# Gate LoRA and twelve head sums as fp32r products of parts, in a hybrid GDN and RWKV-7 decoder block

## The chip, the cores and the metric

The kernel runs on one core of one Trainium2 chip. The core has five engines with an instruction stream each: TensorE (PE in the profile; PEld is its weight load), VectorE (DVE), ScalarE (ACT), GpSimd (POOL) and SyncE (SP, which issues most of the DMAs). The metric is the device time of one execution in microseconds, as the median over several runs. Before the change it is 935.27 us (three runs, 934.57 to 936.5).

## The reference

The program computes one decoder block on 512 tokens of width 1024, all in float32. Two token mixers run in parallel on the same normed input (a gated DeltaNet, "GDN", and an RWKV-7 time mix, eight heads of 64 each), are merged by sigmoid gates, and a ConvGLU channel mixer follows. These are the parts that the change touches:

```python
# RWKV-7 time mix
g = jax.nn.sigmoid(g_lo) @ f32(g2)                     # gate LoRA: 160 -> 512
kk = l2_normalize(heads(k * f32(k_k)))                 # a sum of squares over each head
...
mean = jnp.mean(y, axis=-1, keepdims=True)
var = jnp.mean(jnp.square(y - mean), axis=-1, keepdims=True)
y = ((y - mean) * lax.rsqrt(var + LNX_EPS)).reshape(B, T, RWKV_WIDTH) * f32(lnx_w) + f32(lnx_b)
bonus = jnp.sum(r * k * f32(r_k), axis=-1, keepdims=True) * v   # a sum over each head
return (y + bonus.reshape(B, T, RWKV_WIDTH)) * g
# gated DeltaNet, its end
o = rms_norm(o, onorm_w) * jax.nn.silu(heads(z).astype(jnp.float32))   # a mean of squares over each head
```

## The kernel before, in words

**Layout.** Activations lie transposed: a tile has 128 feature rows and T = 512 tokens as columns. A width of 512 (eight heads of 64) is four such column tiles, counted by `ct`; one tile holds two heads. A sum over a head is therefore a matmul with a 128x128 matrix `ones_bd` that has ones in its two diagonal blocks of 64: every row of the result holds its head's sum.

**Precision.** TensorE multiplies fp32 operands as they are, or "fp32r" operands, which are rounded. Where fp32r is used, an operand is split into parts: `split(hi, lo, src, eng)` lets ScalarE cast `src` to `hi` (L145) and another engine subtract, `lo = src - hi` (L148). A projection's product is then three fp32r matmuls, hi·hi, hi·lo and lo·hi (L186, L189, L190). A head sum has exact ones, so `block_sum` (L168 to L175) needs two, with `hi` (L174) and with `lo` (L175). Before the change `block_sum` is used for the eight sums of the layer norm at the end of the RWKV mixer only, with GpSimd for the subtraction. All other head sums, and the gate LoRA, are fp32 matmuls, each of which shows as two rows of PE in the trace.

**Fills.** The large projections stand in a queue. `fill(n)` puts the next n k-tiles of that queue (three matmuls each, L186 to L190) between the steps of a chain, so that TensorE has work while another engine is at the chain. Weights come by DMA from SyncE into `raw` (two buffers), are cast by ScalarE into `whi` (L145) and subtracted by VectorE into `wlo` (L148), two buffers of each. The adaLN vectors are VectorE reductions over a streamed weight (`wada`, L209), spread over the same time.

**What sets the order.** Every engine runs its own stream in order. The framework lays the program's calls into these streams by its own estimate of when operands are ready, so that an added instruction can move others on its engine and elsewhere. Temporaries come from rings: `tmp(tag)` and `tmp_r(tag)` with the same tag share two buffers ("sq", "sp", "acc", "sg", "rs"), and a third request waits until the first one's readers are done.

**The stages around the change.** (1) Until about 212 us the first projections, the GDN's chunk matrices and a triangular solve (`solve`, L594 and L604 on TensorE, L571 and L573 on VectorE). Just before its last steps the gate's hidden values are passed through a sigmoid, in `sg2` (128 rows) and `sg3` (32 rows; L707 and L708). (2) The GDN recurrence over eight chunks (L774 to L817, about 226 to 300 us): per chunk small products (L181), with VectorE's `cz` (L785), `ck` (L793) and `cs` (L807) and ScalarE's `cv` between them. Between its steps, `more(n)` runs a piece of `prepare()` (L718 to L762), which readies the RWKV operands tile by tile: square of k (L732), head sum (L742), reciprocal root on ScalarE, then products on VectorE and GpSimd (L745 to L758), and the bonus' head sum (L760). (3) Chunk products of RWKV (L843, to 311 us), then the four head sums over the GDN output `go` (L857 to L864), the SiLU of z, the product with it, and the `bg` projection that needs it. (4) The RWKV solve and scan (to 457 us), with fills between. (5) The layer norm loop (L947 to L967, about 458 to 486 us): per tile a sum, a square, a second sum, the scale, and the gate product of two fp32 matmuls: 128 rows of g2 with `sg2` (L963) and 32 rows with `sg3` (L964). (6) Projections to the end.

Of the kernel before, what the change touches and what calls it, by code (L numbers as in the profile page):

```python
# [23 lines left out]
T = 512  # L24
# [31 lines left out]
def body(ctx, tc, io, out, tap=lambda name, ap: None):  # L56
# [298 lines left out]
    p = pa()  # L355
# [59 lines left out]
    lora = ct4(slot(11))  # L415
    lo1, w2, a2, wt = lora[:, 0], lora[0:65, 1], lora[:, 2], lora[0:65, 3]
    sg2 = const.tile([128, T], F32, name="sg2")
    sg3 = const.tile([32, T], F32, name="sg3")
    sp.dma_start(w2, io["w2"])
    sp.dma_start(a2[64:128], io["a2"])  # L420
    pool.memset(wt[64:65], 1.0)
# [22 lines left out]
    p = first_ps[0]  # L444
    ba = tmp("rs")
    act.copy(ba[32:64], p[32:64])
    token_shift(sg3, p, col("mu_lo", 2), omu[:, 14:15], 32)
    for j in range(4):
        gkq(0, j)(first_ps[1 + j])
        if j < 2:  # L450
# [254 lines left out]
    fill(2)  # L705
    table(SIG)
    fn(sg2, sg2, AF.Sigmoid)  # L707
    fn(sg3, sg3, AF.Sigmoid)  # L708
    for b in range(4):
        p = pa()  # L710
        pe.matmul(p, wt[:, 128 * b:128 * b + 128], w2, start=True, stop=True)
# [11 lines left out]
    def prepare():  # L723
        for ct in range(4):
            p = pa()
            pe.matmul(p, a2[64:128, 128 * ct:128 * ct + 128], lo1[64:128], start=True, stop=True)
            fn(aa[:, ct], p, AF.Sigmoid, bias=col("a0", ct))
            yield
        table(EXP)
        for ct in range(4):  # L730
            sq = tmp("sq")
            act.activation(sq, rk_[:, ct], AF.Square, scale=col("k_k", ct))  # L732
            p = pa()
            for b in range(4):
                pe.matmul(p[:, 128 * b:128 * b + 128], lw[:, b, 128 * ct:128 * ct + 128], cumtri,
                          start=True, stop=True)
            pinc, pi = tmp("acc"), tmp("sg")
            fn(pinc, p, AF.Exp)
            fn(pi, p, AF.Exp, scale=-1.0)
            yield  # L740
            p = pa()
            pe.matmul(p, ones_bd, sq, start=True, stop=True)  # L742
            kk = tmp("rs")
            rstd_of(p, 1.0, kk)
            dve.scalar_tensor_tensor(kk, rk_[:, ct], col("k_k", ct), kk, op0=ALU.mult, op1=ALU.mult)  # L745
            pool.tensor_copy(ch(ar[:, 0, ct])[:, :, 0:1], ch(kk)[:, :, 0:1])
            pool.tensor_copy(pend[:, ct], ch(pinc)[:, :, C - 1])
            dve.tensor_tensor(ch(ar[:, 0, ct])[:, :, 1:], ch(kk)[:, :, 1:], ch(pinc)[:, :, 0:C - 1], op=ALU.mult)
            pool.tensor_tensor(kk, aa[:, ct], kk, op=ALU.mult)
            yield  # L750
            t = tmp("sq")
            dve.tensor_scalar(t, aa[:, ct], col("k_a", ct), oka[:, ct:ct + 1], op0=ALU.mult, op1=ALU.add)
            dve.tensor_tensor(rk_[:, ct], rk_[:, ct], t, op=ALU.mult)
            dve.tensor_tensor(aa[:, ct], kk, pi, op=ALU.mult)

            dve.scalar_tensor_tensor(t, rk_[:, ct], col("r_k", ct), rr_[:, ct], op0=ALU.mult, op1=ALU.mult)
            pool.tensor_tensor(rk_[:, ct], pi, rk_[:, ct], op=ALU.mult)
            dve.tensor_tensor(rr_[:, ct], rr_[:, ct], pinc, op=ALU.mult)  # L758
            p = pa()
            pe.matmul(p, ones_bd, t, start=True, stop=True)  # L760
            act.copy(bonus[:, ct], p)
            yield  # L762

# [93 lines left out]
    for ct in range(4):  # L857
        sq = tmp("sq")
        act.activation(sq, go[:, ct], AF.Square)
        p = pa()  # L860
        pe.matmul(p, ones_bd, sq, start=True, stop=True)
        rs = tmp("rs")
        rstd_of(p, 1.0 / C, rs)
        dve.scalar_tensor_tensor(go[:, ct], go[:, ct], col("onorm"), rs, op0=ALU.mult, op1=ALU.mult)  # L864
# [71 lines left out]
    tap("ry", ry)  # L936


    g2s = slot2(2)
    g2a, g2b = g2s[:, 0:T], g2s[0:32, T:2 * T]  # L940
    sp.dma_start(g2a, io["g2"][0:128])
    sp.dma_start(g2b, io["g2"][128:160])
    table(EXP)
    sig_in[0] = False
    rb_h, rb_l = quarter(slot(2, F32R)), quarter(slot(12, F32R))
    for ct in range(4):
# [13 lines left out]
        dve.scalar_tensor_tensor(t, t, col("lnx_w", ct), rs, op0=ALU.mult, op1=ALU.mult)  # L960
        dve.scalar_tensor_tensor(t, t, col("lnx_b", ct), bonus[:, ct], op0=ALU.add, op1=ALU.add)
        p = pa()
        pe.matmul(p, g2a[:, 128 * ct:128 * ct + 128], sg2, start=True, stop=False)  # L963
        pe.matmul(p, g2b[:, 128 * ct:128 * ct + 128], sg3, start=False, stop=True)  # L964
        dve.tensor_tensor(t, t, p, op=ALU.mult)
        split(rb_h[ct], rb_l[ct], t)
        fill(2)  # L967
# [256 lines left out]
```

## Time and profile before

The profiled execution took 937.31 us; its span, from the first to the last instruction, is 935.6 us, at a mean granted clock of 0.983.

| what | before |
|---|---|
| median of the runs | 935.27 us |
| profiled execution, its span | 937.31 us, 935.6 us |
| TensorE busy | 876.3 us (94%), 5459 matmul rows |
| VectorE, ScalarE, GpSimd busy | 533.3, 419.2, 95.2 us |
| fp32 head sums in `prepare()` (L742, L760) | 8, in 232 to 300 us |
| fp32 head sums over `go` (L861) | 4, in 311 to 325 us |
| fp32 gate matmuls (L963, L964) | 8, in 458 to 486 us |

A row of the page's groups or of a view by line has: line, engine, operation, output<-inputs, shape, count | busy us, mean ns of one | idle time of the engine just before, and what ended it. A row of the waits has: engine, what it was about to do <- the engine and instruction that it waited for: us in total, times, longest. A row of the chain or the timeline begins with its start and its length in us. Matmul rows overlap, since TensorE is pipelined; the distance from one start to the next tells what a matmul costs, not its length.

### The profile page before, as it was taken

The page shows a single profiled execution, that of the slowest core. Times are in us where ns is not written, and L with a number is a line of the kernel's source. Part 1 is how long each engine was busy: PE and PEld are TensorE (multiplying, and loading weights), DVE is VectorE, ACT ScalarE, POOL GpSimd, SP SyncE. Part 2 cuts the span into 40 slices and gives each one's busy share as a digit, 9 for nine tenths or more (in the row PEclk, how much of TensorE's full clock was granted, in tenths as well). Part 3 has the DMA queues.
Part 4 walks back from the last instruction along what each step waited for, and adds up shares of the span by engine and source line. Part 5 has one row for each costly group of instructions (what it writes and reads, how often), then busy time and mean ns, then how long its engine had stood idle before and what let it go on. Part 6 is the DMA issues. An engine that isn't in the chain of part 4 may idle for free.

```text
span 935.6 us, 13853 instructions
## 1 busy us (share of the span) xinstructions
PE 876.3 (94%) x5459; PEld 687.7 (74%) x5459; DVE 533.3 (57%) x858; ACT 419.2 (45%) x680; POOL 95.2 (10%) x91
## 2 busy tenths in 40 slices
PE   2999999999989978899999999999999999999996
PEld 1886577677656666677668888888888888888885
DVE  5987859824696786255476537564445445332233
ACT  5367543734554747632465335343333333333231
POOL 1000300000352300001230120000000000010112
PEclk9999999997999989899999999999999999999998
DMA  9841245363323367644546542322322322533322
GB/s 332 283 149 67 91 105 185 109 166 112 103 82 113 69 213 267 162 147 148 183 158 202 171 141 84 111 91 92 109 92 90 105 99 90 179 98 100 107 80 91
DMA packets 81119, 125.72 MB, mean 134 GB/s; under 512 B 26045, under 2 KB 42813, under 8 KB 80990
## 3 DMA queue, kind: packets, MB, share of 16 engines
q1 hardware_dynamic: 81054, 124.83, 42.2%
q8 instruction: 43, 0.70, 0.3%
q14 instruction: 22, 0.18, 0.1%
HBM read 110.13 MB, written 14.16 MB: 133 GB/s over the span
## 4 chain that ended last, share of the span: by engine, by line
PE 69%; DVE 10%; DMA 6%; ACT 6%; issue 6%; POOL 2%; SPq 0%; DVEq 0%; POOLq 0%; ACTq 0%
PE ps_mm L186 19%; PE ps_mm L189 18%; PE ps_mm L190 18%; DMA wada<-in_w_ada 4%; DVE wlo L148 2%; PE ps_pc L181 2%; DVE wada L209 1%; ACT tmp_rs L94 1%; PE ps_pc L186 1%; PE ps_pc L189 1%; PE ps_pc L190 1%; ACT slot L619 1%; PE ps_pa L186 1%; PE ps_pa L189 1%; PE ps_pa L190 1%
## 5 line engine op out<-in xcount | busy, mean ns | idle before, releaser
L186 PE MATMUL ps_mm<-hh,whi 128*128 128x512 f32 (+1 forms) x642 | 264.2, 412 | 9.8 <-ACT hh L308 3.4
L148 DVE TENSOR_TENSOR wlo<-raw,whi 128x1024 fp32r<-128x1024 f32 (+2 forms) x140 | 161.2, 1152 | 176.2 <-ACT whi L145 170.6
L190 PE MATMUL ps_mm<-hh,wlo 128*128 128x512 f32 (+1 forms) x642 | 255.0, 399 | 1.3 <-DVE wlo L148 1.3
L189 PE MATMUL ps_mm<-hl,whi 128*128 128x512 f32 (+1 forms) x642 | 253.8, 396 | 0.0
L145 ACT CAST whi<-raw 128x1024 fp32r<-128x1024 f32 (+2 forms) x140 | 137.1, 979 | 259.7 <-PE ps_mm L189 198.4
L186 PEld LDWEIGHTS ps_mm<-hh,whi 128*128 128x128 f32 x642 | 121.5, 190 | 46.8 <-issue 8.5
L190 PEld LDWEIGHTS ps_mm<-hh,wlo 128*128 128x128 f32 x642 | 121.6, 189 | 31.6 <-issue 3.4
L189 PEld LDWEIGHTS ps_mm<-hl,whi 128*128 128x128 f32 x642 | 122.1, 190 | 26.7 <-issue 4.0
L186 PE MATMUL ps_mm<-slot,whi 128*128 128x512 f32 (+1 forms) x226 | 85.7, 379 | 4.7 <-ACT tmp_sp L94 4.7
L190 PE MATMUL ps_mm<-slot,wlo 128*128 128x512 f32 (+1 forms) x226 | 85.1, 376 | 0.0
L189 PE MATMUL ps_mm<-slotd,whi 128*128 128x512 f32 (+1 forms) x168 | 62.4, 371 | 0.0
L186 PEld LDWEIGHTS ps_mm<-slot,whi 128*128 128x128 f32 x226 | 43.2, 191 | 12.6 <-ACT tmp_sp L94 4.9
L190 PEld LDWEIGHTS ps_mm<-slot,wlo 128*128 128x128 f32 x226 | 43.1, 191 | 7.7
L189 PE MATMUL ps_mm<-slot,whi 128*128 128x512 f32 (+1 forms) x122 | 45.3, 372 | 0.0
L186 PE MATMUL ps_mm<-slotd,whi 128*128 128x512 f32 (+1 forms) x96 | 36.4, 379 | 0.0
L190 PE MATMUL ps_mm<-slotd,wlo 128*128 128x512 f32 (+1 forms) x96 | 36.1, 376 | 0.0
L209 DVE CUSTOM_DVE_ANT_0 wada<-wada,cond,cols 128x512 f32<-128x512 f32 x32 | 25.6, 800 | 18.3 <-DMA wada<-in_w_ada 18.2
L189 PEld LDWEIGHTS ps_mm<-slotd,whi 128*128 128x128 f32 x168 | 31.6, 188 | 5.7
L1099 DVE TENSOR_TENSOR tmp_sg<-tmp_acc,ps_mm 128x512 f32<-128x512 f32 x20 | 13.8, 688 | 36.0 <-PE ps_mm L190 35.8
L209 DVE CUSTOM_DVE_ANT_0 wada<-wada,cond,half 128x512 f32<-128x512 f32 x32 | 24.9, 779 | 14.6 <-DMA wada<-in_w_ada 14.4
L398 DVE SCALAR_TENSOR_TENSOR tmp_acc<-ps_mm,cols,tmp_acc 128x511 f32<-128x511 f32 (+2 forms) x44 | 32.8, 746 | 0.7
L1032 POOL COPY tmp_rs<-tmp_sq 128x512 f32<-128x512 f32 x2 | 2.1, 1064 | 304.0 <-ACT tmp_sq L1029 304.0
(270 smaller groups left out, 1262.5 us busy)
## 6 DMA issues: line engine op xcount, KB each, us to landing
raw<-in_w_in SPq DMA_DIRECT2D x40, 512.0 KB, 4.1
raw<-in_w_fi SPq DMA_DIRECT2D x37, 512.0 KB, 3.5
wada<-in_w_ada SPq DMA_DIRECT2D x64, 256.0 KB, 2.7
raw<-in_w_fo SPq DMA_DIRECT2D x16, 512.0 KB, 3.6
slot<-in_w_ada SPq DMA_DIRECT2D x10, 512.0 KB, 8.5
slot<-in_xT SPq DMA_DIRECT2D x16, 256.0 KB, 4.6
raw<-in_w_out SPq DMA_DIRECT2D x8, 512.0 KB, 3.4
raw<-in_w_in SPq DMA_DIRECT2D x8, 448.0 KB, 4.5
```

The costliest lines, as they stand in the source:

```text
L94: i = act.activation(*a, **k)
L145: i = act.copy(hi, src)
L148: j = eng.tensor_tensor(lo, src, hi.bitcast(F32), op=ALU.subtract)
L181: last["step"] = pe.matmul(*a, **k)
L186: i = pe.matmul(p, hi, xh, start=start, stop=False)
L189: pe.matmul(p, hi, xl, start=False, stop=False)
L190: pe.matmul(p, lo, xh, start=False, stop=stop)
L209: i = dve.tensor_tensor_reduce(out=w, in0=w, in1=cond[:, part], scale=1.0, scalar=half[:, j:j + 1] if u else col("b_ada", j), op0=ALU.mult ...
L398: dve.scalar_tensor_tensor(acc[:, i:], p[:, :T - i], w[:, taps - 1 - i:taps - i], acc[:, i:], op0=ALU.mult, op1=ALU.add)
L619: (act.copy if e == c or quiet else dve.tensor_copy)(place(e, 2 * b + c), p[hs(c), :, e, :])
L1032: pool.tensor_copy(sums[0], sq)
L1099: dve.tensor_tensor(t, accs[j], p, op=ALU.mult)
```

## The change

Three edits. First, the twelve fp32 head sums (four squares and four bonuses in `prepare()`, four over `go`) become `block_sum` with VectorE for the subtraction; the parts live in the rings "sq" or "acc", and "sp". Second, the gate product becomes four fp32r matmuls per tile: three on the 128 rows (hi·hi, hi·lo, lo·hi) and one on the last 32 rows, which are stacked threefold into 96 rows, on one side as hi, hi, lo and on the other as hi, lo, hi, so that one matmul makes the three products. Third, what this needs: `sg3` gets 96 rows with a copy of the sigmoid in rows 64 to 95; the parts of the gate and of g2 are made after the scan's code, g2 comes by four DMAs into one of the two `raw` buffers, the gate's parts take slot 3 and those of g2 take the double slot 2. On the engines this adds 19 operations to ScalarE, 16 to VectorE, takes 20 fp32 matmuls from TensorE and adds 40 fp32r ones.

```diff
-    sg3 = const.tile([32, T], F32, name="sg3")
+    sg3 = const.tile([96, T], F32, name="sg3")
...
-    fn(sg3, sg3, AF.Sigmoid)
+    fn(sg3[0:32], sg3[0:32], AF.Sigmoid)
+    act.copy(sg3[64:96], sg3[0:32])
...
             p = pa()
-            pe.matmul(p, ones_bd, sq, start=True, stop=True)
+            block_sum(p, sq, "sq", dve)
...
             p = pa()
-            pe.matmul(p, ones_bd, t, start=True, stop=True)
+            block_sum(p, t, "sq", dve)
             act.copy(bonus[:, ct], p)
...
         act.activation(sq, go[:, ct], AF.Square)
         p = pa()
-        pe.matmul(p, ones_bd, sq, start=True, stop=True)
+        block_sum(p, sq, "acc", dve)
...
-    g2s = slot2(2)
-    g2a, g2b = g2s[:, 0:T], g2s[0:32, T:2 * T]
-    sp.dma_start(g2a, io["g2"][0:128])
-    sp.dma_start(g2b, io["g2"][128:160])
+    gate_h, gate_l, gate_s, g2_s = quarter(slot(3, F32R))
+    g2p = slot2(2, F32R)
+    g2_h, g2_l = g2p[:, 0:T], g2p[:, T:2 * T]
+    g2_raw = raw_tile()
+    sp.dma_start(g2_raw[:, 0:T], io["g2"][0:128])
+    for k in range(3):
+        sp.dma_start(g2_raw[32 * k:32 * k + 32, T:2 * T], io["g2"][128:160])
+    split(gate_h, gate_l, sg2)
+    for k in range(3):
+        act.copy(gate_s[32 * k:32 * k + 32], sg3[64:96] if k == 2 else sg3[0:32])
+    dve.tensor_tensor(gate_s[64:96], sg3[64:96], gate_s[64:96].bitcast(F32), op=ALU.subtract)
+    act.copy(g2_s[0:96], g2_raw[0:96, T:2 * T])
+    dve.tensor_tensor(g2_s[32:64], g2_raw[32:64, T:2 * T], g2_s[32:64].bitcast(F32), op=ALU.subtract)
+    split(g2_h, g2_l, g2_raw[:, 0:T])
...
         p = pa()
-        pe.matmul(p, g2a[:, 128 * ct:128 * ct + 128], sg2, start=True, stop=False)
-        pe.matmul(p, g2b[:, 128 * ct:128 * ct + 128], sg3, start=False, stop=True)
+        cols_ = slice(128 * ct, 128 * ct + 128)
+        pe.matmul(p, g2_h[:, cols_], gate_h, start=True, stop=False)
+        pe.matmul(p, g2_h[:, cols_], gate_l, start=False, stop=False)
+        pe.matmul(p, g2_l[:, cols_], gate_h, start=False, stop=False)
+        pe.matmul(p, g2_s[0:96, cols_], gate_s[0:96], start=False, stop=True)
```

The change also moves instructions. Line numbers of the changed kernel are one higher from the `sg3` copy (L709) on, and 13 higher in the layer norm loop.

ScalarE before the recurrence, before the change (`sg_462` and `sg_463` are sg2 and sg3, `slot_1363` is `lw`, L402 is the scale of a token shift, L145 a weight cast):

```order
L94 ACTIVATE sg_462<-sg_462 128x512
L94 ACTIVATE sg_463<-sg_463 32x512
L94 ACTIVATE slot_1363<-ps_pa 128x512 x3
L402 ACTIVATE slot_1357<-ps_mm,omu 128x512
L94 ACTIVATE slot_1363<-ps_pa 128x512
L145 CAST whi<-raw 128x1024
```

and with it:

```order
L94 ACTIVATE sg_462<-sg_462 128x512
L94 ACTIVATE sg_463<-sg_463 32x512
L94 ACTIVATE slot_1363<-ps_pa 128x512
L709 COPY sg_463<-sg_463 32x512
L94 ACTIVATE slot_1363<-ps_pa 128x512 x3
L402 ACTIVATE slot_1357<-ps_mm,omu 128x512
L145 CAST whi<-raw 128x1024
```

The copy is new, and the fourth sigmoid of `lw` stands ahead of L402 now. On TensorE, 24 fills that stood before the solve's L594 come after its L604.

VectorE at the end of the recurrence, between its last two `cz`, before the change:

```order
L785 TENSOR_TENSOR cz<-slot_1319,ps_pc 128x256
L793 TENSOR_TENSOR ck<-ps_pc,kdec 128x256
L807 TENSOR_TENSOR cs<-cs,ps_pc 128x256
L209 ISA wada,mod<-wada,cond,half 128x512
L209 ISA mod 128x1
L403 SCALAR_TENSOR_TENSOR slot_1356<-ps_mm,cols,slot_1356 128x511
L148 TENSOR_TENSOR wlo<-raw,whi 128x1024
L785 TENSOR_TENSOR cz<-slot_1319,ps_pc 128x256
```

and the ten rows up to the last `cz` with it (`tmp_sp<-tmp_sq` is a split of the change):

```order
L746 SCALAR_TENSOR_TENSOR tmp_rs<-slot_1357,cols,tmp_rs 128x512
L749 TENSOR_TENSOR slotd_1358<-tmp_rs,tmp_acc 128x8x63
L754 TENSOR_TENSOR slot_1357<-slot_1357,tmp_sq 128x512
L403 SCALAR_TENSOR_TENSOR slot_1356<-ps_mm,cols,slot_1356 128x511
L755 TENSOR_TENSOR slot_1792<-tmp_rs,tmp_sg 128x512
L757 SCALAR_TENSOR_TENSOR tmp_sq<-slot_1357,cols,slotd_1358 128x512
L148 TENSOR_TENSOR wlo<-raw,whi 128x1024
L759 TENSOR_TENSOR slotd_1358<-slotd_1358,tmp_acc 128x512
L148 TENSOR_TENSOR tmp_sp<-tmp_sq 128x512
L786 TENSOR_TENSOR cz<-slot_1319,ps_pc 128x256
```

Before, the fourth tile's products of `prepare()` were done ahead of the last but one `cz`; now they stand between the last two. Seven of the eight splits of `prepare()` lie between the first `cz` and the last.

TensorE in the layer norm loop, first tile, before the change:

```order
L174 MATMUL ps_pa<-tmp_sg,ones_r 128x512
L963 MATMUL ps_pa<-sg_462,slotd_4158 128x512
L175 MATMUL ps_pa<-tmp_sp,ones_r 128x512
L964 MATMUL ps_pa<-sg_463,slotd_4158 128x512
L190 MATMUL ps_mm<-hh_111,wlo 128x512
```

and with it:

```order
L174 MATMUL ps_pa<-tmp_sg,ones_r 128x512
L977 MATMUL ps_pa<-slot_4219,slotd_4220 128x512
L175 MATMUL ps_pa<-tmp_sp,ones_r 128x512
L978 MATMUL ps_pa<-slot_4219,slotd_4220 128x512
L979 MATMUL ps_pa<-slot_4219,slotd_4220 128x512
L980 MATMUL ps_pa<-slot_4219 128x512
L190 MATMUL ps_mm<-hh_111,wlo 128x512
```

One gate matmul still stands between the two halves of the second sum, and three behind it. On SyncE, the loads of x for the residual (L1020) that go into slot 3 come after the last gate product now, since that slot holds the gate's parts until then.

More of the change, by code (lines that the diff above doesn't have):

```diff
@@ L446, in body @@
     act.copy(ba[32:64], p[32:64])
-    token_shift(sg3, p, col("mu_lo", 2), omu[:, 14:15], 32)
+    token_shift(sg3[0:32], p, col("mu_lo", 2), omu[:, 14:15], 32)
     for j in range(4):
```

## The prediction

> **What bounds the kernel now.** I read the page's busy line and the engines' shares of its chain first:
>
> ```profile
> PE 876.3 (94%) x5459; PEld 687.7 (74%) x5459; DVE 533.3 (57%) x858; ACT 419.2 (45%) x680; POOL 95.2 (10%) x91
> ...
> PE 69%; DVE 10%; DMA 6%; ACT 6%; issue 6%; POOL 2%; SPq 0%; DVEq 0%; POOLq 0%; ACTq 0%
> ```
>
> TensorE is busy 94% of the span and is 69% of the chain, so work taken off it looks like gain. But that is an average over stages. The table of busy time by stretch shows where a TensorE microsecond counts:
>
> ```profile
> core 0: us, PE busy (x) PEld busy (x) DVE busy (x) ACT busy (x) POOL busy (x), PEclk, DMA share, GB/s
> 170.00:212.00 42.00, 39.10 (x395) 29.52 (x394) 20.55 (x50) 24.41 (x43) 0.00 (x0) 0.98 0.47 133
> ...
> 245.00:296.00 51.00, 45.92 (x452) 31.37 (x450) 43.75 (x66) 26.45 (x52) 26.35 (x23) 1.00 0.33 99
> ...
> 311.00:325.00 14.00, 12.36 (x50) 8.11 (x45) 9.97 (x15) 11.30 (x22) 7.47 (x4) 1.00 0.39 79
> ...
> 385.00:445.00 60.00, 57.38 (x854) 43.78 (x854) 29.46 (x57) 19.80 (x39) 4.97 (x5) 0.94 0.50 160
> ...
> 458.00:486.00 28.00, 27.68 (x94) 16.61 (x94) 19.61 (x31) 18.52 (x29) 9.72 (x7) 1.00 0.45 142
> ```
>
> The eight sums of `prepare()` run in 245 to 296, beside the GDN recurrence. There VectorE is busy 43.75 of 51 us, nearly as full as TensorE. The four sums over `go` run in 311 to 325, where ScalarE has 11.30 of 14. Only the gate products (458 to 486) stand where TensorE alone is full. The chain of waits inside the recurrence, in order of time, is almost all VectorE and GpSimd:
>
> ```profile
> 260.76 1.75 POOL tmp_rs L749
> ...
> 262.54 0.69 DVE slot L754
> 263.23 0.66 DVE tmp_sq L756
> 263.89 1.13 DVE wlo L148
> 265.02 1.68 DVE slotd L758
> 266.70 0.33 DVE cz L785
> 267.04 1.10 DVE tmp_sq L752
> 268.14 0.66 DVE wada L209
> ```
>
> The recurrence's own step, `cz`, has its turn only when what stands before it in VectorE's stream is done: here a weight split and a product of `prepare()`. So that stage is set by VectorE's order, and the change puts more into it.
>
> **The prices.** TensorE rows first, two fp32 head sums back to back, then the gate products of one column tile and GpSimd's split that runs beside them:
>
> ```profile
> 319.23 1.98 PE L861 MATMUL ps_pa<-tmp_sq,ones_r 128*128 128x512 f32 x4 [1.06 <-ACT tmp_sq L859]
> 320.65 0.80 PE L186 MATMUL ps_mm<-hh,whi 128*128 128x512 f32 x1
> 321.28 0.40 PE L189 MATMUL ps_mm<-hl,whi 128*128 128x512 f32 x1
> 321.52 0.39 PE L190 MATMUL ps_mm<-hh,wlo 128*128 128x512 f32 x1
> 321.75 0.40 PE L186 MATMUL ps_mm<-hh,whi 128*128 128x512 f32 x1
> ...
> 460.40 0.50 PE L174 MATMUL ps_pa<-tmp_sg,ones_r 128*128 128x512 f32 x1
> 460.74 1.02 PE L963 MATMUL ps_pa<-sg,slotd 128*128 128x512 f32 x2
> 461.76 0.50 PE L175 MATMUL ps_pa<-tmp_sp,ones_r 128*128 128x512 f32 x1
> 462.19 1.12 PE L964 MATMUL ps_pa<-sg,slotd 32*128 32x512 f32 x2
> 463.24 0.50 PE L190 MATMUL ps_mm<-hh,wlo 128*128 128x512 f32 x1
> ```
> ```profile
> 460.43 1.28 POOL L148 TENSOR_TENSOR tmp_sp<-tmp_sq,tmp_sg 128x512 fp32r<-128x512 f32 x1 [2.76 <-ACT tmp_sg L145]
> ```
>
> An fp32r matmul of 128x512 takes 0.23 us from start to start (321.52 to 321.75). From 319.23 to 321.28 stand two fp32 sums and one fp32r matmul, so a sum takes (2.05 - 0.23)/2 = 0.91 us. The sum as parts is two fp32r matmuls, 0.46: it saves 0.45, and twelve save 5.4. Of the gate, the 32-row product costs 1.05 to the next start, plus 0.20 by which L175 before it is longer than 0.23: 1.25. Three fp32r matmuls take its place, 0.69, which saves 0.56. The 128-row product (461.76 - 460.74 = 1.02) becomes one of 0.23, saving 0.79. Four column tiles make 4 x 1.35 = 5.4. So **10.8 us of TensorE time** go away in all. What VectorE and ScalarE pay for a sum (minimum, median and maximum in ns of a split and a cast; then ScalarE's copies, as count and mean):
>
> ```profile
> L148 DVE TENSOR_TENSOR slot<-tmp_acc,slot x4: 680/692/693, 468.9 to 488.1; 128x512 fp32r<-128x512 f32 x4
> L145 ACT CAST tmp_sg<-tmp_sq x4: 622/624/626, 459.7 to 480.3; 128x512 fp32r<-128x512 f32 x4
> L761 ACT COPY slot<-ps_pa 128x512 f32<-128x512 f32 x4 | 2.4, 588 | 10.5 <-PE ps_pa L760 10.5
> L816 ACT COPY cv<-cs 64x256 f32<-64x256 f32 x13 | 5.3, 405 | 2.4 <-PE ps_pc L181 0.9 <-DVE cs L807 0.9 <-ACT slot L402 0.4
> ```
>
> A sum whose source is late now takes 0.62 + 0.69 + 0.46 = 1.77 us instead of 0.91: **0.86 longer**, and 0.69 more in VectorE's stream.
>
> **A, before the recurrence.** The third copy of `sg3` and a sigmoid that is moved up stand in ScalarE's order ahead of the next weight cast, and TensorE already waited there once for a weight split, 1.3 us (last column of its row):
>
> ```profile
> L190 PE MATMUL ps_mm<-hh,wlo 128*128 128x512 f32 (+1 forms) x642 | 255.0, 399 | 1.3 <-DVE wlo L148 1.3
> ```
>
> The copy is new work, between 0.41 and 0.59 us by the two copy rows; the sigmoid is only moved. Bounds 0 (the prefetched weights last) and +1.2 (a copy and a sigmoid, about 0.6 each, both on the path); I take the copy, **+0.6**. The 24 fills that TensorE does later in its stream than before cost nothing in themselves: they cover the wait that they are moved to.
>
> **B, the recurrence.** Seven splits lie between the first and the last `cz`: 7 x 0.69 = 4.8 us of VectorE. The other saving there, 8 x 0.45 of TensorE, is not on the path. VectorE's waits in that stretch, the possible cover, are:
>
> ```profile
> DVE slot L754 <- POOL tmp_rs L749: 2.2, 3, 0.9
> DVE cs L807 <- PE ps_pc L181: 1.9, 3, 1.2
> DVE slot L403 <- ACT slot L402: 1.3, 1, 1.3
> DVE ck L793 <- PE ps_pc L181: 1.1, 2, 0.9
> ```
>
> That is 6.5 us, but a split fills a wait only if it stands right before it. Two of these are waits for the recurrence's own products, which get no earlier. A second effect is the ring of temporaries: `sq` has two buffers, and the high part now takes one, so the next tile's square starts only after this tile's second split, where before it had a buffer to itself. And the last `cz` now stands behind the fourth tile's whole `prepare()` work and two splits; before only a `ck`, a `cs`, a wada product, a token shift and a weight split stood between the last two `cz`. Queued behind it are the last chunk's products, the L843 products after them and the sums over `go`. Lower bound 0 (all splits in waits; TensorE's saving behind a late source could take it to -1 at best), upper +4.8 (none) and up to +6 if the ring also stalls. The least the chain pays is the four first sums, at 0.86 each less what their waits cover by half, 1.7; between that and 4.8 I take **+3.2**.
>
> **C, the sums over `go`.** ScalarE gets 4 x 0.62 = 2.5 us in a stretch where 2.7 are free. Behind these sums stand the SiLU of z, the product with it and the `bg` products:
>
> ```profile
> PE ps_mm L186 <- ACT tmp_sp L94: 4.7, 1, 4.7
> ```
>
> TensorE waits 4.7 us there for ScalarE, so its 4 x 0.45 saved are only added to that wait, and the chain to it is longer by one sum, 0.86, up to all four (3.4). The row of the wait is nearer to one, since the earlier sums run beside fills: **+0.8**, bounds 0 and +3.4.
>
> **D, the gate.** The new casts and splits of `gate` and g2 (five ScalarE operations of about 0.6 us, four of VectorE) lie in the scan, where ScalarE has 19.80 and VectorE 29.46 of 60 us: nothing, and about 1 us if g2 came late. The x2 loads, which share a slot with the gate parts, move behind the last gate product; their first use comes after the merge products, so nothing here, 1 us if not. In the loop, the second sum's low part waits for GpSimd: its split ends at 461.71 and L175 starts at 461.76. The fp32 product of 1.02 us filled that wait; the fp32r one leaves a hole, since TensorE cannot pass L175. So the 0.79 is lost to the wait and only the 0.56 behind L175 counts: **-2.3** in four tiles, bounds 0 (the whole chain is GpSimd's) and -5.4.
>
> Sum: 0.6 + 3.2 + 0.8 - 2.3 = **+2.3 us**. The profiled execution shown took 937.31 us with a span of 935.6, so I expect a span near 937.9. The median of the runs is 935.27, which is 2.0 under that execution, so the forecast for the median is **937.6 us**.
>
> **A rule on the other side of the price.** In the stage B rows, GpSimd stretches VectorE: L758, a product of two operands, means 1483 ns there:
>
> ```profile
> L758 DVE TENSOR_TENSOR slotd<-slotd,tmp_acc 128x512 f32<-128x512 f32 x4 | 5.9, 1483 | 0.0
> L757 POOL TENSOR_TENSOR slot<-tmp_sg,slot 128x512 f32<-128x512 f32 x4 | 7.0, 1752 | 6.5 <-DVE tmp_sq L756 4.2 <-DVE cz L785 2.3
> ```
>
> A split is the same kind of operation, 0.69 alone. If each of the seven falls beside a GpSimd product it takes up to 1.48, and B is 10.4 instead of 4.8 at its top. In the new order the split follows L758's product, which takes the blow first; so I hold this for a rival only. [...]
>
> **The rivals.**
> 1. *VectorE has room and TensorE's saving counts where it is full.* For it: the 6.5 us of waits in B and TensorE at 27.68 of 28 in D. Against it: VectorE's chain rows above. B at 0, C at 0, A at 0.6, D near its end, -4.6: 4.0 less, 931.3 us. If all 10.8 count, 924.5.
> 2. *A wash.* The splits are half absorbed (B +1.6), the rest as forecast: 0.6 + 1.6 + 0.3 - 2.3 = +0.2, 935.5 us.
> 3. *The splits meet GpSimd's products, slower still.* In B, before the last `cz`: from the point where three of seven splits fall beside GpSimd, 3 x 0.79 = 2.4 more; with D halved by the GpSimd wait (-1.1) it is 0.6 + 5.6 + 0.8 - 1.1 = +5.9, 941.2 us. For it: L758's row; against it: the order.
> 4. *The change does not do what it says*, TensorE time stays: nothing speaks for it, since the fp32 rows above are plainly longer.
>
> **How the numbers follow.** A measurement of this kernel tells a change from none at about 0.2%, 1.9 us. Chances: forecast 0.42 (own range 936 to 940), rival 1 0.25 (of it 0.03 for the full saving), rival 2 0.21, rival 3 0.12. Faster is rival 1 and a little of the wash, 0.27; same is the rest of the wash and the forecast's low edge, 0.26; slower is what is left, 0.47. The range reaches from rival 1 to rival 3: 931.5 to 942.
>
> **What would show each step.** The seven `cz` of before (first and last start):
>
> ```profile
> L785 DVE TENSOR_TENSOR cz<-slot,ps_pc x7: 406/408/417, 235.2 to 296.2; 128x256 f32<-128x256 f32 x7
> ```
>
> B: the last `cz` starts 2 to 5 us later after the first than these 61.0 us, and VectorE's busy time between 245 and 300 rises by about 5 us. C: the wait of L186 for the z gate's ScalarE stays at 4 us or more. D: the four tiles take some 2 us less, and L175 waits for GpSimd four times by 0.5 us or more. A: a wait of L190 for a weight split between 170 and 200 that is longer than 1.3. If the last `cz` is no later, B is wrong and rival 1 holds; if the loop of D is shorter by 5 us, the GpSimd wait was no limit.

## The result

The changed kernel takes 951.33 us (median, 949.53 to 951.78) against 934.92 us before: a ratio of 1.0163, with a 95% interval of 1.0137 to 1.0189. That is 16.4 us slower, where 2.3 us slower were forecast and 942 was the upper end of the range. One execution of a kernel below, the one with the gate edit alone, took 1236 us at a granted clock of 0.656; it is left out of that kernel's median, and its profile, which was taken in that execution, is not read. The page of the changed kernel, its span and busy time:

```profile
span 950.1 us, 13894 instructions
...
PE 880.6 (93%) x5459; PEld 696.4 (73%) x5459; DVE 542.0 (57%) x874; ACT 428.3 (45%) x699; POOL 93.8 (10%) x91
```

TensorE has less to do and is still busy 4.3 us longer than before (880.6 against 876.3): its mean granted clock fell from 0.983 to 0.969. The rest of the 14.5 us is 10.2 us more of idle TensorE. An estimate from these figures: (1 - 0.983) x 935.6 = 15.9 us of full clock were lost before and (1 - 0.969) x 950.1 = 29.5 us after, so the slower clock ate some 13.6 us of TensorE time, more than the 10.8 that the change takes off it. When the same instructions start in the two profiled executions, counted from the first L711 product (L712 after the change; 174.5 us before, 173.4 after), this shows where the time went:

| start of | before, us | after, us | later by | added in the stage |
|---|---|---|---|---|
| the first `cz` | 60.7 | 64.5 | 3.8 | 3.8 (A) |
| the last `cz` | 121.7 | 130.1 | 8.4 | 4.6 (B) |
| the last chunk product (L843, now L844) | 136.4 | 148.5 | 12.1 | 3.7 (behind B) |
| the last scale of `go` (L864) | 149.5 | 164.4 | 14.9 | 2.8 (C) |
| the last SiLU product (L873) | 157.3 | 171.1 | 13.8 | -1.1 |
| the last product with the gate | 312.3 | 327.1 | 14.8 | 1.0 (scan and D) |
| the last residual scale (L1027) | 751.1 | 767.0 | 15.9 | 1.1 |

The table of busy time by stretch of the changed kernel, with the granted clock behind the busy times:

```profile
core 0: us, PE busy (x) PEld busy (x) DVE busy (x) ACT busy (x) POOL busy (x), PEclk, DMA share, GB/s
165.00:193.00 28.00, 25.55 (x98) 17.72 (x97) 21.05 (x53) 19.74 (x35) 0.00 (x0) 0.94 0.48 139
...
204.00:219.00 15.00, 14.32 (x226) 10.75 (x220) 4.58 (x8) 7.14 (x12) 0.00 (x0) 0.54 0.28 90
...
238.00:300.00 62.00, 53.09 (x529) 37.22 (x528) 46.12 (x79) 35.62 (x69) 22.74 (x23) 1.00 0.28 87
300.00:311.00 11.00, 10.16 (x68) 7.64 (x69) 5.62 (x10) 3.67 (x9) 3.39 (x2) 0.53 0.28 83
...
322.00:338.00 16.00, 10.73 (x46) 7.76 (x43) 13.17 (x19) 11.53 (x24) 6.90 (x4) 1.00 0.33 67
472.00:501.00 29.00, 25.06 (x99) 17.93 (x100) 19.38 (x29) 18.26 (x29) 9.83 (x8) 1.00 0.45 142
```

and of the kernel before, behind the solve and behind the recurrence:

```profile
208.00:223.00 15.00, 14.32 (x220) 10.65 (x213) 4.59 (x8) 6.94 (x12) 0.00 (x0) 0.66 0.35 107
...
296.00:311.00 15.00, 13.91 (x286) 10.82 (x286) 9.29 (x25) 8.86 (x25) 0.00 (x0) 1.00 0.28 87
```

In the recurrence TensorE is idle 8.9 of 62 us. Behind it, from 300 to 311, it runs at a clock of 0.53; the kernel before ran at 1.00 there (296 to 311). In the sums over `go` it is busy 10.7 of 16 us. In the gate's loop it is busy 25.1 of 29 us, where it was full before (27.68 of 28): the saving is there, as idle time. What TensorE waited for in these three stages (recurrence, sums over `go`, gate loop):

```profile
PE ps_pa L174 <- ACT tmp_sq L145: 2.5, 3, 1.7
PE ps_pa L175 <- DVE tmp_sp L148: 2.5, 3, 1.2
PE ps_pc L181 <- DVE ck L794: 2.2, 3, 1.0
...
PE ps_pa L175 <- DVE tmp_sp L148: 3.4, 1, 3.4
...
PE ps_pa L175 <- POOL tmp_sp L148: 4.0, 6, 1.0
```

The new waits are for the parts themselves: the cast (L174 waits for it) and the subtraction (L175).

### The profile page after: what moved, and what is told of

Its sections match the earlier page's. It is cut to its first block, busy times and chain, and to the rows that moved or that the text cites. A ratio compares the mean times of both kernels' runs of the same rounds, so it can differ in the third digit from the quotient of the medians.

```text
span 950.1 us, 13894 instructions
## 1 busy us (share of the span) xinstructions
PE 880.6 (93%) x5459; PEld 696.4 (73%) x5459; DVE 542.0 (57%) x874; ACT 428.3 (45%) x699; POOL 93.8 (10%) x91
## 4 chain that ended last, share of the span: by engine, by line
PE 66%; DVE 12%; ACT 6%; DMA 6%; issue 6%; POOL 2%; SPq 0%; DVEq 0%; POOLq 0%; ACTq 0%
PE ps_mm L186 18%; PE ps_mm L190 17%; PE ps_mm L189 17%; DMA wada<-in_w_ada 4%; PE ps_pc L181 2%; DVE wlo L148 2%; ACT slot L619 1%; ACT tmp_rs L94 1%; DVE wada L209 1%; PE ps_pc L186 1%; PE ps_pc L189 1%; PE ps_pc L190 1%; DVE slot L573 1%; PE ps_pa L186 1%; DVE pr L571 1%
## 5 line engine op out<-in xcount | busy, mean ns | idle before, releaser
L186 PE MATMUL ps_mm<-hh,whi 128*128 128x512 f32 (+1 forms) x642 | 264.9, 413 | 9.5 <-ACT hh L308 3.4
L190 PE MATMUL ps_mm<-hh,wlo 128*128 128x512 f32 (+1 forms) x642 | 257.2, 402 | 2.3 <-DVE wlo L148 2.3
L148 DVE TENSOR_TENSOR wlo<-raw,whi 128x1024 fp32r<-128x1024 f32 (+2 forms) x140 | 158.9, 1135 | 170.9 <-ACT whi L145 164.5
L145 ACT CAST whi<-raw 128x1024 fp32r<-128x1024 f32 (+2 forms) x140 | 137.0, 979 | 260.9 <-PE ps_mm L189 195.4
L186 PEld LDWEIGHTS ps_mm<-hh,whi 128*128 128x128 f32 x642 | 123.3, 192 | 46.6 <-issue 5.6
L190 PEld LDWEIGHTS ps_mm<-hh,wlo 128*128 128x128 f32 x642 | 123.0, 192 | 31.6 <-DVE wlo L148 4.1
L186 PE MATMUL ps_mm<-slot,whi 128*128 128x512 f32 (+1 forms) x226 | 85.8, 380 | 4.6 <-ACT tmp_sp L94 4.6
L190 PE MATMUL ps_mm<-slot,wlo 128*128 128x512 f32 (+1 forms) x226 | 85.1, 377 | 0.1
L186 PEld LDWEIGHTS ps_mm<-slot,whi 128*128 128x128 f32 x226 | 43.1, 191 | 12.9 <-ACT tmp_sp L94 4.8
L190 PEld LDWEIGHTS ps_mm<-slot,wlo 128*128 128x128 f32 x226 | 43.0, 190 | 8.8 <-DVE wlo L148 1.2
L186 PE MATMUL ps_mm<-slotd,whi 128*128 128x512 f32 (+1 forms) x96 | 36.4, 379 | 0.0
L190 PE MATMUL ps_mm<-slotd,wlo 128*128 128x512 f32 (+1 forms) x96 | 36.1, 376 | 0.0
L1115 DVE TENSOR_TENSOR tmp_sg<-tmp_acc,ps_mm 128x512 f32<-128x512 f32 x20 | 13.8, 688 | 35.6 <-PE ps_mm L190 35.5
L94 ACT ACTIVATE tmp_acc<-tmp_acc 128x512 f32<-128x512 f32 x22 | 13.9, 632 | 41.5 <-DVE tmp_acc L398 41.4
```

Of the source, the lines that this page charges most:

```text
L94: i = act.activation(*a, **k)
L145: i = act.copy(hi, src)
L148: j = eng.tensor_tensor(lo, src, hi.bitcast(F32), op=ALU.subtract)
L186: i = pe.matmul(p, hi, xh, start=start, stop=False)
L190: pe.matmul(p, lo, xh, start=False, stop=stop)
L1115: dve.tensor_tensor(t, accs[j], p, op=ALU.mult)
```

## The experiments

**The four edits apart.** Four kernels, run together on one chip beside the kernel before (935.63 us there). The first has the gate edit alone, the second the twelve sums alone, the third and fourth the sums of `prepare()` and those over `go` alone. For example the third against before:

```diff
-            pe.matmul(p, ones_bd, sq, start=True, stop=True)
+            block_sum(p, sq, "sq", dve)
...
-            pe.matmul(p, ones_bd, t, start=True, stop=True)
+            block_sum(p, t, "sq", dve)
```

> The gate edit alone, with all twelve head sums left as fp32 matmuls. Theory (the sums make the loss; the gate gains nothing because each second sum's low part is still waited for, 3.5 us of waits for GpSimd in the trace after): within 2 us of before, 934 to 937 us. Rival (the gate edit's own pieces, the copy of sg3 and the order of the solve, start the loss): 938 us or more, with the clock at half in 184 to 188 us as in the changed kernel.

> The twelve head sums alone, the gate left as two fp32 matmuls per tile. Theory: nearly the whole loss, 947 to 952 us, and the recurrence from first to last cz takes 64 us or more. Rival: half of the loss or less, 942 us or below.

> Only the eight sums of prepare(). Theory (VectorE's splits and the ring of temporaries hold up the recurrence, and TensorE's idle time there halves its clock behind it): 8 to 12 us over before, 943 to 947 us. Rival (the sums over go carry the larger part): below 940 us.

> Only the four sums over go. Theory: 2 to 4 us over before (the stretch from the end of the chunk products to the last scaled go was 2.7 us longer in the changed kernel), 937 to 939 us. Rival (hidden in the wait for the SiLU of z): 934 to 936 us.

| kernel | median, us | ratio to before, 95% interval |
|---|---|---|
| gate edit alone | 939.99 | 1.0046 (1.0029 to 1.0062) |
| twelve sums alone | 946.91 | 1.0123 (1.0106 to 1.0140) |
| eight sums of `prepare()` alone | 942.20 | 1.0075 (1.0060 to 1.0090) |
| four sums over `go` alone | 941.30 | 1.0065 (1.0050 to 1.0080) |

The three pieces nearly add: 0.46 + 0.75 + 0.65 = 1.86% against 1.63% for all. The theory of the first expectation fell and its rival holds, as far as the time goes: the gate edit makes more than a quarter of the loss. The twelve sums and those of `prepare()` came out just under their ranges; over `go` the loss is 6 us where the theory had 2 to 4.

**A: the place of one copy.** The gate edit alone again, with the copy of `sg3` written beside the gate's other parts. On ScalarE it then comes behind the sigmoids and the first L402.

```diff
-    act.copy(sg3[64:96], sg3[0:32])
...
     split(gate_h, gate_l, sg2)
+    act.copy(sg3[64:96], sg3[0:32])
```

> The gate edit alone, with the copy of sg3 into rows 64 to 95 written with the gate's other parts, so that on ScalarE it stands behind the sigmoids and the token shift's L402 and not ahead of them. Theory A (the copy delays the weight casts before the recurrence, and the 1 to 2 us that TensorE idles there cost it its clock): 3 us or more of the gate edit's loss of 4 us go, 934 to 937 us. Rival (the copy's place does not matter; the gate's parts or the later x2 loads cost the time): 939 to 941 us.

936.35 us against 935.05, ratio 1.0008 (0.9994 to 1.0022): the whole loss of the gate edit is gone, and the first `cz` starts 60.5 us behind the first L711, as it did before (60.7). The early copy also moved the fills, and they are back: from the first L711 to the solve's L604, TensorE has 112 fill matmuls here, 111 before and 87 in the changed kernel. So what is shown is that the copy's place costs the time, together with the order that it brings; a moved copy with unmoved fills was not run. What happened shows in TensorE's timeline of the changed kernel:

```profile
180.88 0.39 PE L190 MATMUL ps_mm<-hh,wlo 128*128 128x512 f32 x1
181.83 0.50 PE L186 MATMUL ps_mm<-hh,whi 128*128 128x512 f32 x1 [0.56 <-ACT whi L145]
182.18 0.39 PE L189 MATMUL ps_mm<-hl,whi 128*128 128x512 f32 x1
183.69 0.50 PE L190 MATMUL ps_mm<-hh,wlo 128*128 128x512 f32 x1 [1.12 <-DVE wlo L148]
...
184.84 0.63 PE L186 MATMUL ps_mm<-hh,whi 128*128 128x512 f32 x1
185.26 0.63 PE L189 MATMUL ps_mm<-hl,whi 128*128 128x512 f32 x1
```

Two waits, 0.56 and 1.12 us, for a weight cast and its split that came late; 1 us later a matmul starts every 0.43 us and not every 0.23, until 187.8. Before, TensorE had one such wait there, of 0.8 us, and its granted clock was 1.00 from 165 to 193. The half clock behind the solve is longer too: 0.54 over the 15 us from 204, where the kernel before had 0.66 over the 15 us from 208. The second of these is only seen beside the first; it was not tried alone. By the granted clocks, (1 - 0.94) x 28 = 1.7 us of full clock were lost from 165 to 193 and (0.66 - 0.54) x 15 = 1.8 us more than before behind the solve; these 3.5 us, an estimate, are nearly the 3.8 by which the first `cz` is late. The two waits ahead of the stretch sum to 1.7 us; how long a wait has to be for the clock to fall, no run here shows.

**D: GpSimd's wait in the gate loop.** As the last kernel, with VectorE for the loop's low parts; and later VectorE's low parts on the kernel before, without the gate edit.

```diff
-        block_sum(p, y, "sg")
+        block_sum(p, y, "sg", dve)
...
-        block_sum(p, sq, "sg")
+        block_sum(p, sq, "sg", dve)
```

> As the one before, and the layer norm loop's low parts are subtracted by VectorE (0.69 us) and not by GpSimd (1.29 us and more). Theory D (L175's wait for GpSimd eats what the gate's fp32r products save): the wait shrinks and 2 to 4 us are gained, 931 to 934 us. Rival (the loop is bound by its chain through ScalarE and VectorE whatever the splitter): within 1 us of the run before.

> The kernel before, with VectorE and not GpSimd for the low parts in the layer norm loop; the gate stays fp32. If the 3 us gained with the gate edit belong to both together: within 1 us of before, 934 to 936 us. If they belong to VectorE's low parts alone: 931 to 933 us.

The first takes 932.33 us, ratio 0.9971 (0.9961 to 0.9982): **faster than before**, and 4 us faster than with GpSimd. The second takes 935.83, ratio 0.9990 (0.9977 to 1.0003): no difference by the median, though three of its ten runs took 931.72 to 933.43, as little as the first. So the gate edit is worth about 3 us, but only where nothing waits in its place, and by the medians VectorE's low parts are worth that only with it. TensorE's waits in the loop, of the gate edit with GpSimd and then with VectorE:

```profile
PE ps_pa L175 <- POOL tmp_sp L148: 4.5, 6, 1.0
```
```profile
PE ps_mm L186 <- ACT slot L94: 0.7, 1, 0.7
```

With GpSimd, TensorE waits 4.5 us in the loop, of the 5.4 us saved (0.7 us before the change). With VectorE that wait is gone.

**C: what holds up the sums over `go`.** VectorE and then GpSimd in the kernel with only these sums, in order of time:

```profile
314.59 0.69 DVE L148 TENSOR_TENSOR tmp_sp<-tmp_sq,tmp_acc 128x512 fp32r<-128x512 f32 x1
315.20 2.61 DVE L864 SCALAR_TENSOR_TENSOR slotd<-slotd,cols,tmp_rs 128x512 f32<-128x512 f32 x1
317.73 2.60 DVE L148 TENSOR_TENSOR tmp_sp<-tmp_sq,tmp_acc 128x512 fp32r<-128x512 f32 x1
```
```profile
314.75 2.51 POOL L852 TENSOR_SCALAR_AFFINE_SELECT slotd<-slotd 64x2048 f32<-64x2048 f32 x1
317.33 2.45 POOL L852 TENSOR_SCALAR_AFFINE_SELECT slot<-slot 64x2048 f32<-64x2048 f32 x1
```

A split of 0.69 us takes 2.60 and a scale of 0.75 takes 2.61. Each starts while a select of GpSimd runs and ends 0.55 us after that select (317.81 against 317.26, 320.33 against 319.78). TensorE waits 3.6 us for the split at L175. Before, the same selects held up a weight split (1.86 us in place of 1.2) and a scale (L864, 2.60 us), but no matmul waited for VectorE there (TensorE's waits from 311 to 325 are for ScalarE, 1.1 and 0.5 us).

Three ways to take the split away from the selects. First the loop moved ahead of the chunk products, where GpSimd has nothing to do (busy 0.00 us from 296 to 311 before), without and with the sums as parts:

```diff
     for _ in prep:
         fill(1)
+    for ct in range(4):
+        sq = tmp("sq")
+        act.activation(sq, go[:, ct], AF.Square)
+        ...
```

> The kernel before, with the loop of the four sums over go (still fp32) moved ahead of the chunk products L843. A control for the next run: within 2 us of before, 934 to 937 us, by the theory that only VectorE's part beside GpSimd's L852 selects costs time there.

> As the one before, with the four sums over go as parts. Theory (in their old place two splits or scales of VectorE stand beside GpSimd's L852 select for 2.6 us each, which makes the loss of 5.7 us; here GpSimd is idle): within 1.5 us of the control. Rival (the chain of a sum is longer by its split wherever it stands): 3 us or more over the control.

941.89 and 942.09 us (ratios 1.0069 and 1.0074). The control itself loses 6.8 us, so its expectation fell: the move delays the chunk products (the last one starts 148.0 us behind the first L711, 136.4 before). But on top of it the four sums as parts cost 0.2 us, with splits of 0.69 us. Second, the two selects written behind the SiLU of z:

> The four sums over go as parts in their old place, with GpSimd's two L852 selects moved behind the SiLU of z and its splits (they are needed only by the scan). Theory (the loss of 5.7 us is VectorE held up by these selects): a split takes 0.69 us each, and the time is within 1.5 us of before, 934 to 937 us. Rival (the loss is the longer chain of a sum): 939 us or more, with splits of 0.69 us all the same.

> The gate edit with its late copy and VectorE for the layer norm's low parts (932.3 us alone), together with the four sums over go as parts and the selects L852 moved back. Theory: the sums over go cost nothing then, 931 to 934 us. Rival: the chain of the sums costs 3 us or more, 935 us and above.

942.66 us (1.0082) and 938.84 us (1.0038): no gain. GpSimd has little else to do there (in the first, busy 9.8 of the 110 us from 290 to 400), so the selects still ran when their data were ready, beside the same splits (mean 1325 ns in the first, as in the kernel with only these sums), and TensorE waited 3.6 us at L175 in both. These two runs say nothing on the cause. Third, the selects held back by a dependence, without and with the sums as parts:

```diff
+        act.copy(sa_[e][hs(1 - e)][:, 0, 0:1], go[hs(1 - e), 3, 0:1])
         d = sa_[e][hs(1 - e)].rearrange("p h (c t) -> p h c t", c=NC)
         pool.affine_select(out=d, in_=d, ...)
```

> The kernel before (fp32 sums) with GpSimd's two L852 selects held back until the last scaled go is there: a copy of 64 elements from it goes into a column that the select overwrites with zero. A control for the next run. Theory: the two scales L864 take 0.75 us each and not 1.6; the selects now lie beside the SiLU's products: within 2 us of before, 934 to 938 us.

> As the control, with the four sums over go as parts. Theory (the selects hold up the splits): TensorE's wait of 3.6 us at L175 shrinks below 1 us and the sums cost at most 1.5 us over the control. Rival (the longer chain of a sum): 4 us or more over the control.

938.18 us (1.0025, 1.0014 to 1.0037) and 938.65 us (1.0035, 1.0021 to 1.0049). The sums as parts cost 0.5 us over the control, the wait at L175 is gone, and splits and scales have their own length again (the second kernel, in its fastest run, 936.42 us):

```profile
L860 DVE SCALAR_TENSOR_TENSOR slotd<-slotd,cols,tmp_rs 128x512 f32<-128x512 f32 x4 | 3.0, 748 | 1.0 <-ACT tmp_rs L94 1.0
...
L148 DVE TENSOR_TENSOR tmp_sp<-tmp_sq,tmp_acc 128x512 fp32r<-128x512 f32 x3 | 2.1, 689 | 0.3 <-ACT tmp_acc L145 0.3
```

The control itself is 2.6 us over before, since the SiLU's products now stand beside the selects (two of them take 4.52 us together, where one takes 0.69). So the loss of C is the selects' hold on VectorE, not the longer chain of a sum. The sums do not gain either: the wait for the SiLU's chain behind them takes what TensorE saves (7.9 us, 6.1 in the control), as the prediction said.

**B: the sums of `prepare()`.** Seven of the eight; only the first sums; only the bonus sums:

```diff
-            pe.matmul(p, ones_bd, t, start=True, stop=True)
+            if ct == 3:
+                pe.matmul(p, ones_bd, t, start=True, stop=True)
+            else:
+                block_sum(p, t, "sq", dve)
```

> Seven of the eight sums of prepare() as parts; the bonus sum of the fourth tile stays fp32. Theory (clock): with all eight, TensorE waits 1.7 us for the last sum's high part and then runs at half clock for 6 to 8 us; the fp32 sum waits less and the clock stays, so this one sum is worth 2.5 to 4 us and the time is 938 to 940 us. Rival (VectorE's and ScalarE's extra operations alone make the loss, evenly): 0.8 us less than all eight, 941 to 942 us.

> Only the four first sums of prepare() (squares of k) as parts. Theory (they stand on each tile's chain, 0.86 us longer each, and add 2.8 us to VectorE before the last cz): last cz 1.5 to 3 us later after the first than the 61 us of before, 936 to 939 us. Rival (they are covered): no later, 934 to 936 us.

> Only the four bonus sums of prepare() as parts. Theory (a TensorE stream that waits at L175 is what costs, wherever the sum stands): 2 us or more over before, 937 to 941 us. Rival (only the first sums, on each tile's chain, cost): within 1 us of before.

| sums as parts | median, us | ratio to before, 95% interval |
|---|---|---|
| all eight | 942.20 | 1.0075 (1.0060 to 1.0090) |
| seven, the last bonus not | 941.64 | 1.0067 (1.0048 to 1.0086) |
| the four first sums | 941.33 | 1.0069 (1.0052 to 1.0086) |
| the four bonus sums | 943.14 | 1.0083 (1.0058 to 1.0108) |

The loss does not follow the number of splits: four cost as much as eight. The expectation of the first sums was too low (the last `cz` starts 64.9 us behind the first, 61.0 before), that of the bonus sums too (937 to 941), and that the last sum alone is worth 2.5 to 4 us fell.

Is it the clock? In its profiled execution the kernel with the bonus sums has half clock three times within the recurrence. The first of them, then a stretch of the kernel with seven sums (the first column is the stretch, the one behind the busy times the granted clock):

```profile
264.00:268.00 4.00, 2.48 (x16) 1.80 (x18) 4.00 (x6) 1.68 (x4) 2.32 (x2) 0.85 0.40 131
268.00:272.00 4.00, 4.00 (x21) 1.98 (x17) 0.75 (x3) 2.03 (x5) 1.26 (x1) 0.50 0.24 66
```
```profile
244.00:248.00 4.00, 2.34 (x34) 1.46 (x34) 3.73 (x8) 1.53 (x4) 1.39 (x2) 1.00 0.55 163
248.00:252.00 4.00, 3.73 (x40) 2.92 (x35) 4.00 (x5) 1.95 (x5) 2.05 (x3) 1.00 0.12 43
```

After 1.5 us of idle TensorE in 4 us the clock is halved in the first; after 1.7 us it is not in the second, which had a clock of 1.00 there and from 276 to 324. But that profile of the bonus sums is of the slowest of their four runs (946.43 us, mean clock 0.972); the others took 941.35 to 943.17 at 0.980 and 0.981, where the kernel before has 0.981 at the median. With seven sums and with the four first sums the median clock is no lower than before (0.983 and 0.982), and they lose 6 us all the same. With all eight it is 0.978: (0.981 - 0.978) x 940 = 2.8 us of their 6.6, an estimate. So the clock is at most a part of this loss.

Then the two halves of a sum's load. In the first kernel casts and splits are made but nobody reads them, and the sums stay fp32. In the second there is the cast but no split; its low part is left out and the high part summed twice.

```diff
+            split(tmp_r("sq"), tmp_r("sp"), sq)
             pe.matmul(p, ones_bd, sq, start=True, stop=True)
```

> The eight sums of prepare() as fp32 matmuls as before, but the casts and splits are made all the same, into the same rings, and nobody reads them. Theory (TensorE's wait at L174 and L175 is what costs): at most 3 us over before, 935 to 939 us. Rival (the load of 8 casts and 8 splits, and the rings, make the loss): 941 us or more.

> The eight sums of prepare() as two fp32r matmuls of the cast high part; the low part is left out, so the sums are those of rounded values. Theory (half of the waits are for the split, half for the cast; VectorE has its old load): between, 937 to 940 us. Rival (without the split all is covered): within 1 us of before or faster.

941.77 us (1.0066, 1.0044 to 1.0087) and 939.06 us (1.0046, 1.0027 to 1.0064). My theory at that point, that TensorE's new waits at L174 and L175 make the loss, fell: without them it is nearly all still there. Casts and splits that nobody reads are enough. Without the splits about 3.3 us are left by the median; that kernel also has the cheaper matmuls, so this is not the price of the casts alone.

Where these kernels lose the time shows in the starts of `cz`, from one to the next, in their profiled executions:

| sums as parts | steps from `cz` to `cz`, us | first to last |
|---|---|---|
| none (before) | 10.6, 10.6, 10.2, 8.3, 12.9, 8.4 | 61.0 |
| all eight | 10.5, 10.8, 8.3, 10.2, 11.1, 13.9 | 64.8 |
| seven | 10.8, 10.8, 8.3, 10.2, 11.1, 13.2 | 64.5 |
| the four first sums | 10.4, 10.2, 10.9, 5.9, 19.2, 8.3 | 64.9 |
| the four bonus sums | 10.5, 10.2, 11.8, 12.6, 15.0, 11.1 | 71.3 |
| parts made, nobody reads them | 10.7, 10.2, 15.1, 11.1, 9.4, 10.1 | 66.6 |
| casts without splits | 10.4, 10.3, 12.1, 8.8, 10.4, 10.8 | 62.8 |

The last step, before and with all eight sums:

```profile
287.80 0.41 DVE L785 TENSOR_TENSOR cz<-slot,ps_pc 128x256 f32<-128x256 f32 x1
...
296.20 0.41 DVE L785 TENSOR_TENSOR cz<-slot,ps_pc 128x256 f32<-128x256 f32 x1
```
```profile
284.39 0.42 DVE L785 TENSOR_TENSOR cz<-slot,ps_pc 128x256 f32<-128x256 f32 x1 [0.86 <-PE ps_pc L181]
...
298.25 0.41 DVE L785 TENSOR_TENSOR cz<-slot,ps_pc 128x256 f32<-128x256 f32 x1
```

With all eight sums the first five steps take 50.9 us, less than before (52.6), although five splits lie in them. The last step takes 13.9 us and not 8.4: the fourth tile's VectorE work of `prepare()` now stands there, which was done one step earlier before. With the four first sums the step of 19.2 us holds most of the third tile's work and all of the fourth's. So a cast or a split may cost time because the framework lays the streams out differently around it, and this order is a rival to the load. It is not the whole answer: with the bonus sums VectorE's order is that of before with four splits put in, and the time is lost all the same (the 71.3 us are of their slowest run). No run adds all eight parts in the old order or takes the new order with fp32 sums.

VectorE's load alone explains little. With all eight sums seven splits take 5.7 us between the first and the last `cz`, but VectorE is busy only 1.5 us longer there (49.5 against 48.0), since other operations got shorter. The three L752, for example, take 0.54 us each and not 1.39; before, all three ran beside GpSimd's L883, and in the changed kernel, where they take the same 0.54, none does.

ScalarE's waits are another candidate. First those of the kernel with all eight sums, then one of before, then TensorE's wait in the kernel where nobody reads the parts:

```profile
ACT tmp_sq L145 <- DVE tmp_sq L756: 8.1, 4, 3.3
ACT tmp_sq L732 <- DVE tmp_sp L148: 5.1, 3, 2.3
```
```profile
ACT slot L761 <- PE ps_pa L760: 10.5, 4, 2.9
```
```profile
PE ps_pa L743 <- ACT tmp_sq L732: 3.1, 3, 1.9
```

The cast of a bonus' source waits for VectorE's L756, 8.1 us in all; but before, ScalarE waited 10.5 us at that place for the sum. The recurrence's own copies `cv` stand behind these casts, yet the longest of the waits (3.3 us) makes a `cv` only 0.3 us late. The other wait is new: the next tile's square (L732) waits for this tile's split, since the ring "sq" has two buffers and the parts use one, 5.1 us in three waits. It is nearly the same with all eight sums, with seven, with the bonus sums alone (5.0) and where nobody reads the parts (4.5), which would fit a loss that does not follow the number of splits; with the four first sums it is 2.4, and without the splits it is gone. Where nobody reads the parts TensorE in turn waits 3.1 us for that square. A ring of its own for the parts was not tried, so the ring's price is not shown. Open are the shares of order, ring and clock in the 6 to 7 us.

## Why the prediction was wrong, step by step

- **What bounds the kernel**: right in kind. In 245 to 296 and in 311 to 325 TensorE's saving was worth nothing, and the sum of 10.8 us of TensorE time was not to be had. The direction was right, the size wrong by a factor of seven. By the kernels with one edit each and their variants, A cost 3.6 us, B 6.6, C 5.7 and D nothing, 15.9 in sum; the forecast had 0.6, 3.2, 0.8 and -2.3. All four terms were too low, so this is no single slip.
- **The clock** is the first thing that is missing. The prediction quotes clocks of 0.94 to 1.00, names none of them as a price, and prices every wait at its length. In A (0.54 and a stretch at 0.57 from 184 to 188) and behind the recurrence (0.53 from 300 to 311) waits of 1.3 to 1.7 us in sum were followed by several microseconds at about half clock.
- **A**, forecast +0.6 with 1.2 as the upper bound: +3.6 by the two gate kernels (939.99 with the early copy, 936.35 with the late one). The place was right, and the failed step is "the copy is new work, between 0.41 and 0.59": the copy's length was taken for its price. "The 24 fills ... cost nothing in themselves" belongs to the same step and is not shown: they moved with the copy, and behind the solve the clock was lower. The 1.3 us of the quoted L190 row is of the whole run; from 165 to 200 it was 0.8 before.
- **B**, forecast +3.2: 6.6 alone. The last `cz` is later by 4.6 us in the changed kernel, within the 2 to 5 named, and 2.8 to 3.7 more come behind it (with all eight sums alone, and in the changed kernel). The step that failed is the price, "7 x 0.69 = 4.8 us of VectorE" less what its waits cover: VectorE's busy time between 245 and 300 did not rise by 5 us, it fell from 45.1 to 43.6, and from the first to the last `cz` it rose by 2.1. That the 4.6 us lie near the forecast is therefore luck in part. What the runs show in its place is a last step of 13.9 us and not 8.4, with the fourth tile's work in it, and a new wait of 5.1 us for the ring. The prediction named both, the ring with "up to +6", but gave the new place no price of its own; the shares of the two stay open. Rival 3's mechanism, splits beside GpSimd, is small here: the split means 811 ns against 692.
- **C**, forecast +0.8: +6 alone. The step that failed is "the chain to it is longer by one sum, 0.86": what made the loss is a split of 2.60 us beside a select of GpSimd, for which TensorE waits 3.6 us. That GpSimd stretches VectorE was in the prediction, with the row of L758 (1483 ns) for it, but asked of B only; GpSimd's 7.47 us in the quoted row of 311 to 325 stood there unasked.
- **D**, forecast -2.3: nothing (1.0008 with the late copy). That GpSimd's wait eats the saving was right; that 0.56 per tile behind L175 escapes it was wrong. What is earlier for TensorE only meets the next wait of the same kind: 4.5 us in six waits against 0.7 in two before. The bound of 0 was named. (The parts of the gate take six ScalarE operations, not five; they cost nothing, as said.)
- **Rival 1** (the saving counts) is refuted for the change as it stands, though a part of its saving on D comes once the wait is taken away: 932.33 us, 2.7 less than before where it had 4.6.
- Of the other signs, the wait of L186 for the z gate (4 us or more forecast, 4.6 measured) and the waits of L175 for GpSimd (four of 0.5 us or more) came as said. The four tiles of D take 0.9 us less, not 2 (28.5 to 27.6 from the first L951 to the last product with the gate). The wait of L190 before the recurrence was to be longer than 1.3 and was 1.12; it grew from 0.8, and the 0.56 for the cast ahead of it is new.

## What to carry to other kernels

Splitting an operand into parts moves work from the engine that is full to two that run in order and have waits of their own. The length of the cast and the subtraction is not the price: in C it was what GpSimd's selects did to a split (2.60 us, 0.69 alone), in A what the copy's place did to the weights behind it and to the order, and in B the order and the ring are the candidates. Before such a change, look at each stage for the second-busiest engine, for GpSimd instructions that overlap the new VectorE work, and for operations that the new order moves across a step of the chain. And where a matmul was the cover of a wait, making it shorter gained nothing here until the wait itself was shortened: the gate edit alone is worth nothing (936.35 us against 935.05), with VectorE's subtraction it is worth 3 us (932.33).

## What the hardware showed that I had not expected

- TensorE's clock halved after waits that were short: 0.56 and 1.12 us within 2.4 us (181.3 to 183.7), then 3 us of matmuls every 0.43 us; and a wait of 1.7 us for a cast ahead of the 0.53 from 300 to 311. It is no rule of these figures alone: with seven sums TensorE idled 1.7 of 4 us (244 to 248) and kept its clock.
- In the kernel with only the sums over `go`, two VectorE operations that met GpSimd's selects each ended 0.55 us after the select did: 2.60 and 2.61 us in place of 0.69 and 0.75.
- Added work can leave an engine's busy time almost as it was: 5.7 us of splits made VectorE busy only 1.5 us longer between the first and the last `cz`, in good part since three L752 took 0.54 us each and not the 1.39 of before, when they ran beside GpSimd's L883.
